# A float32 network on one core: the two token tiles of the stationary pages interleaved word by word

## The chip, the cores and the metric

The kernel runs on one core of one Trainium2 chip. The metric is the device time of one execution in microseconds (us), lower is better. A change of this kernel's time can be told from none from about 2% on.

## The reference, cut to what matters

One sequence of 256 tokens with 1024 channels, all in float32, goes through a state space layer, a causal attention layer, and twice through a mixing layer (latent attention, convolution, retention, gated and merged) and a feed-forward layer. Nearly all the arithmetic is products of the 256 tokens with weight matrices:

```python
h = rms_norm_2(x, ln_mix_pre[l])
proj = h @ w_in[l]                                   # 1024 x 7584
...
merged = gates[:, :, 0] * y_mla + gates[:, :, 1] * y_conv + gates[:, :, 2] * y_ret
x = x + rms_norm_2(merged @ w_out[l], ln_mix_post[l])
h = rms_norm_2(x, ln_ffn_pre[l])
f = (jax.nn.silu(h @ ffn_w_gate[l]) * (h @ ffn_w_up[l])) @ ffn_w_down[l]   # hidden width 2816
x = x + rms_norm_2(f, ln_ffn_post[l])
```

## The kernel before

**Split products.** A float32 operand is split into hi, rounded to the tensor engine's float32r format by ScalarE's copy, and lo, what is left, by a subtraction on VectorE. A product is the sum of three matmuls (`mm3`, lines 163 to 167):

```python
nc.tensor.matmul(out, xh, wh, start=first, stop=False)
nc.tensor.matmul(out, xh, wl, start=False, stop=False)
nc.tensor.matmul(out, xl, wh, start=False, stop=last)
```

The second argument, a block of 128 channels x 128 tokens of the transposed activations, is the stationary operand, which a weight load puts into the array ahead of each matmul. The third, 128 channels x up to 512 columns of a weight matrix, is the moving one, and the result is 128 tokens x 512 columns in PSUM.

**Stationary pages.** `pages` (L214) allots a pair of 4 KB pages (hi, lo) for each four blocks of 128 channels, `[128, 4, 256]`: in each partition 256 tokens follow each other, so a block's 128 tokens of one token tile t are 512 adjacent bytes. The pages are written by `split` (L186 to L194: the hi by ScalarE, L190 or L193, the lo by VectorE, L191 or L194), mostly from `transposed` (L196), which transposes four blocks into PSUM and splits them, with a gain per channel (one split per block, 128 columns wide) or without one (one split for four blocks, 512 wide). `prenorm` (L221) does so with gains at the head of five stages. Names in the trace: xTh/xTl, fh/fl, oTh/oTl, cTh/cTl, mcTh/mcTl, s5mh/s5ml. The state space layer's s5gh/s5gl are pages too, but moving operands (`gemm_t`, L454 to L456); they are written with a step of four words at L844 and L845.

**Weights.** `wtile` (L142) brings 256 x 512 weights by a DMA of 512 KB from SP's queue (raw), splits them (L158 ScalarE, L160 VectorE), and returns a hi and a lo tile. `wbuf` (L135) hands out four buffers of each kind that the whole kernel has, and from the attention stage on two more hi and two more lo that the stage has, by turns.

**Order.** `gemm` (L169) goes through the weight tiles of a product of 512 columns; for each tile it issues 12 matmuls (two token tiles x two k blocks x three), then `pump` runs pieces of side work from queues of closures (attention, convolution taps, retention). `out_rows` (L241) does the same for a product whose 1024 columns are held at once. The unsplit float32 products of the first stage are `gemm_raw` (L428): the trace shows each as two instructions.

Of the kernel before, what the change touches and what calls it, by code (L numbers as in the profile page):

```python
# [23 lines left out]
C = 512  # L24
# [26 lines left out]
class Net:  # L51
# [16 lines left out]
    def stage(self, pages, temps, raws=0, halves=0):  # L68
        """pages and temporaries of a stage; what an earlier stage had is given back."""
# [15 lines left out]
    def page(self, shape, name, dt=F32):  # L85
        """up to 4 KB of each partition"""
        assert int(np.prod(shape[1:])) <= 1024, shape
        return self.bp.tile(shape, dt, tag="q4", name=self.nm(name))
# [46 lines left out]
    def wbuf(self, tag):  # L135
        """buffer of a tile of weights; the stage may have some more of them"""
# [32 lines left out]
    def gemm(self, xs, W, c0, ncols, evac, pts=None):  # L169
        """rows: out[t] = x @ W[:, c0:c0+ncols]; xs: list over k blocks of (hi, lo) aps [128, 256]."""  # L170
        KB = len(xs)
        pts = [self.acc(), self.acc()]
        for k0 in range(0, KB, KT):
            kn = min(KT, KB - k0)
            hi, lo = self.wtile(W[k0 * 128:(k0 + kn) * 128, c0:c0 + ncols], kn, ncols)
            for t in range(2):
                for k in range(kn):
                    xh, xl = xs[k0 + k]
                    s = slice(t * 128, t * 128 + 128)
                    self.mm3(pts[t][:, :ncols], xh[:, s], xl[:, s], hi[:, k, :ncols], lo[:, k, :ncols],  # L180
                             k0 + k == 0, k0 + k == KB - 1)
# [4 lines left out]
    def split(self, dh, dl, src, scale=None):  # L186
        """dh + dl = src * scale, src in PSUM."""
# [8 lines left out]
    def transposed(self, t, row, pages, nb, gains=None, scale=None):  # L196
        """row [128 tok, nb*128] -> split blocks of pages, scaled per channel by gains."""
        nc = self.nc
        for b0 in range(0, nb, 4):
# [4 lines left out]
            s = slice(t * 128, t * 128 + 128)  # L204
            dh, dl = pages[b0 // 4]
            if gains is None:
                self.split(dh[:, :bn, s], dl[:, :bn, s],
                           pt[:, :bn * 128].rearrange("p (b n) -> p b n", b=bn), scale)
            else:
                for b in range(bn):  # L210
                    self.split(dh[:, b, s], dl[:, b, s], pt[:, b * 128:(b + 1) * 128],
                               gains[:, b0 + b:b0 + b + 1])

    def pages(self, nb, name="xT"):  # L214
        return [(self.page([128, min(4, nb - b), 256], name + "h", F32R), self.page([128, min(4, nb - b), 256], name + "l", F32R))
                for b in range(0, nb, 4)]

    def blocks(self, pages):
        return [(h[:, b, :], l[:, b, :]) for h, l in pages for b in range(h.shape[1])]
# [21 lines left out]
    def out_rows(self, xs, W, x, post, out=None):  # L241
        """x + rms(xs @ W) * post, or x + xs @ W when post is None; the first 128 rows are done some tiles ahead."""
# [8 lines left out]
        def product(t, n, k0, kn, hi, lo):  # L251
            s = slice(t * 128, t * 128 + 128)
            for k in range(kn):
                xh, xl = xs[k0 + k]
                self.mm3(pts[t][n], xh[:, s], xl[:, s], hi[:, k, :], lo[:, k, :], k0 + k == 0, k0 + k == KB - 1)
# [36 lines left out]
    def rsqrt1(self, v):  # L292
        """-1024 / 27 / sqrt(v) of a column, by a step of third and one of second order."""
# [16 lines left out]
    # ------------------------------------------------------------------ consts  # L310
# [25 lines left out]
    def sincos(self, out_c, out_s, ang, tag, after=None):  # L336
        """sin and cos of ang (any size that float32 reduces), ang [128, ...]"""
# [18 lines left out]
    def tables2(self):  # L356
# [8 lines left out]
        self.cs = self.sp.tile([128, 2, 2, 80], F32, tag="cs", name="cs", bufs=1)  # (cos/sin, t, mla16|ret64)  # L365
# [5 lines left out]
        # log gammas: min(x, 0) - log1p(exp(-|x|)), log1p by the atanh series  # L371
# [20 lines left out]
        # distances: [m part, mt, n]: relu(n - m), relu(m - n)  # L392
# [9 lines left out]
    # ------------------------------------------------------------------ first block: state space layer  # L402
    def raw_tiles(self, W, c0, ncols, KB):
        """sources of the tiles of gemm_raw, in its order"""
        return [W[k0 * 128:(k0 + KT) * 128, c0 + n0:c0 + n0 + C] for k0 in range(0, KB, KT) for n0 in range(0, ncols, C)]

    def load_raw(self):
        """next tile of self.todo, in any of the buffers of a tile of weights"""
# [6 lines left out]
    def gemm_raw(self, xs, ncols, evac, after=None):  # L415
        """gemm_t on float32 operands that are not split, where the tensor engine has the time: a closure for each tile of self.pre."""
# [22 lines left out]
    def gemm_t(self, xs, W, c0, ncols, evac, order=None):  # L439
        """columns: out^T = W[:, c0:c0+ncols]^T x^T, evac(block, psum [128, 256]); order of the pairs of k blocks."""  # L440
# [20 lines left out]
    def s5_params(self, after):  # L461
# [10 lines left out]
        # powers of ab: [ri, pair, k], k = 0..4  # L472
# [18 lines left out]
        # one chunk further, on (re, -im): [[a, b], [-b, a]] of ab^4  # L491
# [5 lines left out]
        # f = (ab - 1) / (lr + i li)  # L497
# [15 lines left out]
        # sums for products in three multiplications  # L513
# [4 lines left out]
    def s5_bc(self):  # L518
# [4 lines left out]
        # B~ = f B  # L523
# [20 lines left out]
    def s5_pows(self):  # L544
        """powers 1..16 of ab^4: (-im, re, im), pair, power."""
# [19 lines left out]
    def cprod(self, eng, q, l0, Z, Zx):  # L565
        """ab^l z for pairs 8q..8q+7, l = l0..l0+3, as (k1, k2, k3): re = k1 + k3, im = k1 + k2."""
# [14 lines left out]
    def s5_w(self, q, eng):  # L581
        """pairs 8q..8q+7 of ab^k B~, k = 1..4, [(g2, p), qq, (q2, k, c)], pair = 2 qq + q2, re and im."""
# [7 lines left out]
    def s5_wt(self, W, q, w, after=None):  # L590
        """their lhsT [(q2, k, c), qq, (g2, p)]"""
# [8 lines left out]
    def s5_c(self, cab, q, eng):  # L600
        """pairs 8q..8q+7 of [(g2, p), pair, (l, c')] of C ab^l, l = 0..3, re and im."""
# [4 lines left out]
    def s5(self, x_in):  # L606
# [6 lines left out]
        # normalised input; gains go on its channels after the transposes  # L613
# [6 lines left out]
        # gains go on the channels of the input; 1 / rms on what comes out of the first product and on what goes into the second  # L620
# [47 lines left out]
        # block diagonal B~ (re, -im) and the zeros before the kernel taps  # L668
# [55 lines left out]
        # chunk inputs X = W u: [(g2, p), (re, -im), pair, 1 + j], replaced by the states after each chunk  # L724
# [14 lines left out]
        # scan over the 64 chunks: inside 4 groups of 16, across the groups, then what each group takes over  # L739
# [28 lines left out]
        # kernel taps K[l] = Re(C ab^l B~): [(q4, g2, c), pg, (l, c')], channels in order; spread to lower triangles  # L768
# [702 lines left out]
```

## Time and profile before

| what | value |
|---|---|
| runs shown | 1278.69 and 1280.73 us, median 1279.71 |
| span of the profiled execution | 1276.7 us, 3.0 us under the median of the runs |
| TensorE busy (matmuls; weight loads beside them) | 1235.7 us; 1029.5 us |
| VectorE, ScalarE, GpSimd busy | 948.3, 652.9, 51.8 us |
| mean granted TensorE clock | 0.981 |
| HBM read | 205.83 MB, 164 GB/s over the span |

The span goes from the first to the last instruction of the one execution that the profiler recorded. A matmul's recorded duration holds its whole way through the array; the ends are modelled, and matmuls overlap, so their pace is the distance from start to start. PE are the matmuls, PEld the weight loads, DVE is VectorE, ACT ScalarE, POOL GpSimd.

### The profile page before, as it was taken

The numbers are of one execution on the slowest core, as the hardware profiler recorded it, in microseconds if no ns is written. First come the engines' busy times: TensorE is split into PE (matmuls) and PEld (weight loads), VectorE is DVE, ScalarE is ACT, GpSimd is POOL, SyncE is SP. The second block draws the span as 40 slices with busy tenths as digits, with TensorE's granted clock in tenths as the row PEclk, the third lists the DMA queues.
The fourth block names the chain that finished last, engine by engine and source line by source line (L and its number), as shares of the span: only waits on it lengthen the run. The fifth ranks groups of instructions, "written<-read, shape, count | busy, mean of one in ns | idle before, by whom it ended". The sixth has DMA issues, their size and how long they took to land.

```text
span 1276.7 us, 17877 instructions
## 1 busy us (share of the span) xinstructions
PE 1235.7 (97%) x6520; PEld 1029.5 (81%) x6520; DVE 948.3 (74%) x1923; ACT 652.9 (51%) x1073; POOL 51.8 (4%) x42
## 2 busy tenths in 40 slices
PE   7898799999999999999999999999999999999997
PEld 6787777787888888888788887888888887888886
DVE  6999489887889998857755555899998857755544
ACT  3112467675765544544644444666545445644432
POOL 3920000000000000000000000000000000000000
PEclk9779899999999999999999999999999999999999
DMA  9326656644454554555566564544554554665661
GB/s 319 83 43 99 166 174 209 192 136 137 142 164 138 161 161 152 164 201 179 189 180 184 171 235 151 175 134 147 166 159 153 179 184 148 218 190 161 193 211 50
DMA packets 125367, 210.60 MB, mean 165 GB/s; under 512 B 22112, under 2 KB 31328, under 8 KB 125280
## 3 DMA queue, kind: packets, MB, share of 16 engines
q1 hardware_dynamic: 117056, 204.24, 50.9%
q10 hardware_dynamic: 8224, 5.23, 2.1%
q8 instruction: 51, 0.84, 0.3%
q14 instruction: 36, 0.29, 0.1%
HBM read 205.83 MB, written 3.60 MB: 164 GB/s over the span
## 4 chain that ended last, share of the span: by engine, by line
PE 79%; DVE 13%; ACT 3%; DMA 3%; issue 2%; SPq 0%; DVEq 0%; ACTq 0%
PE mm L165 23%; PE mm L167 23%; PE mm L166 22%; DVE lo L160 2%; PE sm L203 2%; ACT hi L158 1%; PE sm L1119 1%; PE sm L1211 1%; DVE cacc L957 1%; PE sm L1094 1%; DVE s5pr L745 1%; PE sm L733 1%; DVE cm L586 1%; DVE s5pr L759 1%; PE mm L455 1%
## 5 line engine op out<-in xcount | busy, mean ns | idle before, releaser
L160 DVE TENSOR_TENSOR lo<-raw,hi 128x1024 fp32r<-128x1024 f32 (+2 forms) x372 | 440.1, 1186 | 235.8 <-ACT hi L158 234.4
L158 ACT ACTIVATE hi<-raw 128x1024 fp32r<-128x1024 f32 (+2 forms) x372 | 382.6, 1032 | 377.8 <-PE mm L167 290.4
L165 PE MATMUL mm<-hi,xTh 128*128 128x512 f32 (+2 forms) x1152 | 451.1, 394 | 1.6 <-ACT xTh L193 1.5
L167 PE MATMUL mm<-hi,xTl 128*128 128x512 f32 (+2 forms) x1152 | 443.7, 386 | 0.3 <-DVE t L297 0.2
L166 PE MATMUL mm<-lo,xTh 128*128 128x512 f32 (+2 forms) x1152 | 443.3, 385 | 0.2 <-DVE lo L160 0.2
L165 PEld LDWEIGHTS mm<-hi,xTh 128*128 128x128 f32 x1152 | 216.4, 188 | 48.9 <-ACT xTh L193 7.3
L167 PEld LDWEIGHTS mm<-hi,xTl 128*128 128x128 f32 x1152 | 216.3, 188 | 46.2 <-DVE t L297 1.5
L166 PEld LDWEIGHTS mm<-lo,xTh 128*128 128x128 f32 x1152 | 216.7, 188 | 41.2 <-DVE lo L160 0.5
L957 DVE SCALAR_TENSOR_TENSOR cacc<-aT,colp,cacc 128x256 f32<-128x256 f32 x240 | 104.2, 476 | 0.0
L165 PE MATMUL mm<-hi,fh 128*128 128x512 f32 x176 | 69.0, 392 | 0.0
L166 PE MATMUL mm<-lo,fh 128*128 128x512 f32 x176 | 68.9, 392 | 0.0
L167 PE MATMUL mm<-hi,fl 128*128 128x512 f32 x176 | 68.8, 391 | 0.0
L167 PEld LDWEIGHTS mm<-hi,fl 128*128 128x128 f32 x176 | 33.0, 187 | 7.4
L165 PEld LDWEIGHTS mm<-hi,fh 128*128 128x128 f32 x176 | 33.0, 188 | 7.3
L166 PEld LDWEIGHTS mm<-lo,fh 128*128 128x128 f32 x176 | 33.0, 188 | 7.2
L277 DVE SCALAR_TENSOR_TENSOR pg<-mm,post 128x512 f32<-128x512 f32 x16 | 11.0, 690 | 21.9 <-ACT pg L275 21.9
L194 DVE SCALAR_TENSOR_TENSOR xTl<-sm,colp,xTh 128x128 fp32r<-128x128 f32 x80 | 24.3, 345 | 3.5 <-ACT xTh L193 3.1
L454 PE MATMUL mm<-s5gh,hi 128*128 128x256 f32 x64 | 19.0, 305 | 7.1 <-ACT s5gh L844 7.1
L193 ACT ACTIVATE xTh<-sm,colp 128x128 fp32r<-128x128 f32 x80 | 24.4, 381 | 1.8 <-DVE xTl L194 1.7
L895 ACT ACTIVATE pg<-mm,t 128x512 f32<-128x512 f32 x24 | 16.5, 690 | 16.9 <-PE mm L167 16.9
L733 PE MATMUL sm<-s5U,s5W 64*64 64x64 f32 x256 | 21.2, 300 | 2.5 <-DMA s5U<-s5ud 2.5
L733 PEld LDWEIGHTS sm<-s5U,s5W 64*64 64x64 f32 x256 | 20.8, 207 | 3.2 <-issue 3.2
(387 smaller groups left out, 1513.2 us busy)
## 6 DMA issues: line engine op xcount, KB each, us to landing
raw<-in_w_in SPq DMA_DIRECT2D x112, 512.0 KB, 3.5
raw<-in_ffn_w_down SPq DMA_DIRECT2D x44, 512.0 KB, 3.8
raw<-in_ffn_w_gate SPq DMA_DIRECT2D x40, 512.0 KB, 3.7
raw<-in_ffn_w_up SPq DMA_DIRECT2D x40, 512.0 KB, 3.6
raw<-in_attn_w_in SPq DMA_DIRECT2D x32, 512.0 KB, 4.3
raw<-in_ret_w_o SPq DMA_DIRECT2D x16, 512.0 KB, 3.2
raw<-in_w_out SPq DMA_DIRECT2D x16, 512.0 KB, 3.2
raw<-in_ssm_w_glu SPq DMA_DIRECT2D x8, 512.0 KB, 4.9
```

Of the source, the lines that this page charges most:

```text
L158: nc.scalar.activation(h, r, AF.Copy)
L160: self.last_lo = nc.vector.tensor_tensor(l, r, h.bitcast(F32), op=ALU.subtract)
L165: nc.tensor.matmul(out, xh, wh, start=first, stop=False)
L166: nc.tensor.matmul(out, xh, wl, start=False, stop=False)
L167: nc.tensor.matmul(out, xl, wh, start=False, stop=last)
L193: a = nc.scalar.activation(dh, src, AF.Copy if isinstance(scale, float) else AF.Identity, scale=scale)
L194: self.last_split = a, nc.vector.scalar_tensor_tensor(dl, src, scale, dh.bitcast(F32), op0=ALU.mult, op1=ALU.subtract)
L203: nc.tensor.transpose(pt[:, b * 128:(b + 1) * 128], row[:, (b0 + b) * 128:(b0 + b + 1) * 128], self.ident)
L454: nc.tensor.matmul(o, wh, xh, start=first and b % 2 == 0, stop=False, skip_group_check=True)
L733: lx[q] = nc.tensor.matmul(pt[g * 64:g * 64 + 64, qq * 64:qq * 64 + 64], Wl[i][h][r, qq, g * 64:g * 64 + 64], U[r, 8 * h + qq, g, :], star ...
L895: nc.scalar.activation(gate[t, n], p, AF.Tanh, scale=hf(t))
L957: nc.vector.scalar_tensor_tensor(cacc[:, b, :], src, sc, cacc[:, b, :], op0=ALU.mult, op1=ALU.add)
```

## The change

A stationary page is now allotted as `[128, nb, 128, 2]` and seen as `[128, nb, 2, 128]`: word 2n of a block is token n of tile 0, word 2n + 1 token n of tile 1. A block of one token tile is 128 words with a step of two words over 1024 bytes, in the weight loads that read it, in ScalarE's and VectorE's writes, and where VectorE reads the hi again. Size and number of the pages are as before. The pages that are moving operands (s5gh, s5gl) keep the old layout by a helper of their own. The rest of the diff removes comments.

```diff
 def gemm(self, xs, W, c0, ncols, evac, pts=None):
...
                 for k in range(kn):
                     xh, xl = xs[k0 + k]
-                    s = slice(t * 128, t * 128 + 128)
-                    self.mm3(pts[t][:, :ncols], xh[:, s], xl[:, s], hi[:, k, :ncols], lo[:, k, :ncols],
+                    self.mm3(pts[t][:, :ncols], xh[:, t], xl[:, t], hi[:, k, :ncols], lo[:, k, :ncols],
                              k0 + k == 0, k0 + k == KB - 1)
...
 def transposed(self, t, row, pages, nb, gains=None, scale=None):
...
-                self.split(dh[:, :bn, s], dl[:, :bn, s],
+                self.split(dh[:, :bn, t], dl[:, :bn, t],
                            pt[:, :bn * 128].rearrange("p (b n) -> p b n", b=bn), scale)
             else:
                 for b in range(bn):
-                    self.split(dh[:, b, s], dl[:, b, s], pt[:, b * 128:(b + 1) * 128],
+                    self.split(dh[:, b, t], dl[:, b, t], pt[:, b * 128:(b + 1) * 128],
                                gains[:, b0 + b:b0 + b + 1])
 
 def pages(self, nb, name="xT"):
-        return [(self.page([128, min(4, nb - b), 256], name + "h", F32R), self.page([128, min(4, nb - b), 256], name + "l", F32R))
-                for b in range(0, nb, 4)]
+        return [(self.stationary(min(4, nb - b), name + "h"), self.stationary(min(4, nb - b), name + "l")) for b in range(0, nb, 4)]
+
+    def stationary(self, nb, name):
+        return self.page([128, nb, 128, 2], name, F32R).rearrange("p b n t -> p b t n")
+
+    def moving(self, nb, name):
+        return [tuple(self.page([128, min(4, nb - b), 256], name + p, F32R) for p in "hl") for b in range(0, nb, 4)]
 
     def blocks(self, pages):
-        return [(h[:, b, :], l[:, b, :]) for h, l in pages for b in range(h.shape[1])]
+        return [(h[:, b], l[:, b]) for h, l in pages for b in range(h.shape[1])]
...
 def out_rows(self, xs, W, x, post, out=None):
...
         def product(t, n, k0, kn, hi, lo):
-            s = slice(t * 128, t * 128 + 128)
             for k in range(kn):
                 xh, xl = xs[k0 + k]
-                self.mm3(pts[t][n], xh[:, s], xl[:, s], hi[:, k, :], lo[:, k, :], k0 + k == 0, k0 + k == KB - 1)
+                self.mm3(pts[t][n], xh[:, t], xl[:, t], hi[:, k, :], lo[:, k, :], k0 + k == 0, k0 + k == KB - 1)
...
 def s5(self, x_in):
...
-        gT = self.pages(8, "s5g")
+        gT = self.moving(8, "s5g")
...
-            mh, ml = (a[:, b % 4, :] for a in mT[b // 4])
-            self.split(mh, ml, m, 0.25)
+            self.split(*(a[:, b % 4] for a in mT[b // 4]), m.rearrange("p (t n) -> p t n", t=2), 0.25)
...
 def conv(self, l, xs, W, hf):
...
-            self.split(cT[0][0][:, 2 * b2:2 * b2 + 2, :], cT[0][1][:, 2 * b2:2 * b2 + 2, :], v)
+            self.split(*(a[:, 2 * b2:2 * b2 + 2] for a in cT[0]), v.rearrange("p b (t n) -> p b t n", t=2))
...
 def mla(self, l, parts):
...
-            self.split(oT[0][0][:, s, :], oT[0][1][:, s, :], pt.rearrange("p (b n) -> p b n", b=2))
+            self.split(oT[0][0][:, s], oT[0][1][:, s], pt.rearrange("p (b t n) -> p b t n", b=2, t=2))
```

## Rows read from the trace of the kernel before

**Rows 1.** The profile page: busy time of each engine (busy us, share of the span, instructions), then the chain that ended last by engine and by line.
```profile
PE 1235.7 (97%) x6520; PEld 1029.5 (81%) x6520; DVE 948.3 (74%) x1923; ACT 652.9 (51%) x1073; POOL 51.8 (4%) x42
...
PE 79%; DVE 13%; ACT 3%; DMA 3%; issue 2%; SPq 0%; DVEq 0%; ACTq 0%
PE mm L165 23%; PE mm L167 23%; PE mm L166 22%; DVE lo L160 2%; PE sm L203 2%; ACT hi L158 1%; PE sm L1119 1%; PE sm L1211 1%; DVE cacc L957 1%; PE sm L1094 1%; DVE s5pr L745 1%; PE sm L733 1%; DVE cm L586 1%; DVE s5pr L759 1%; PE mm L455 1%
```

**Rows 2.** Groups of instructions with shapes kept apart, all of the span: line, engine, operation, out<-in, array tile, out<-in shape, count | busy us, mean ns of one | idle before. L165 alone is shown; L166 and L167 have the same counts.
```profile
L165 PE MATMUL mm<-hi,xTh 128*128 128x512 f32 x1056 | 421.9, 401 | 1.1 <-ACT xTh L193 1.0
...
L165 PE MATMUL mm<-hi,fh 128*128 128x512 f32 x176 | 69.0, 392 | 0.0
...
L165 PE MATMUL mm<-hi,xTh 128*128 128x256 f32 x64 | 18.1, 284 | 0.0
...
L165 PE MATMUL mm<-hi,oTh 128*128 128x512 f32 x32 | 13.1, 410 | 0.0
...
L165 PE MATMUL mm<-hi,s5mh 128*128 128x512 f32 x32 | 12.8, 403 | 0.1
L165 PE MATMUL mm<-hi,cTh 128*128 128x512 f32 x32 | 12.7, 397 | 0.0
...
L165 PE MATMUL mm<-hi,mcTh 128*128 128x512 f32 x16 | 6.3, 391 | 0.0
```

**Rows 3.** Timeline of TensorE from 637 to 654 us, in the first feed-forward stage: start us, us, engine, line, operation, out<-in, array tile, moving shape, count. Of the 70 rows the first, the 46th and the last; the rows between are one matmul each.
```profile
637.49 0.39 PE L165 MATMUL mm<-hi,xTh 128*128 128x512 f32 x1
...
647.69 0.39 PE L165 MATMUL mm<-hi,xTh 128*128 128x512 f32 x1
...
653.29 0.39 PE L165 MATMUL mm<-hi,xTh 128*128 128x512 f32 x1
```

**Rows 4.** The same timeline from 725 to 732 us, where the feed-forward stage's last chunk is 256 columns wide. The first pair of rows is 30 matmuls apart, the second 20.
```profile
725.21 0.28 PE L167 MATMUL mm<-hi,xTl 128*128 128x256 f32 x1
...
728.81 0.28 PE L167 MATMUL mm<-hi,xTl 128*128 128x256 f32 x1
728.92 0.28 PE L165 MATMUL mm<-hi,xTh 128*128 128x256 f32 x1
...
731.19 0.28 PE L167 MATMUL mm<-hi,xTl 128*128 128x256 f32 x1
```

**Rows 5.** Timeline of TensorE from 12 to 17 us, with rows merged: the unsplit float32 products of the first stage (start of the first, us to the end of the last, count). Under it the busy times from 12 to 16 us (start:end, us, busy of PE, PEld, DVE, ACT, POOL with counts, granted clock, DMA share, GB/s).
```profile
12.55 3.62 PE L428 MATMUL mm<-s5x,hi 128*128 128x256 f32 x16
16.00 1.24 PE L428 MATMUL mm<-s5x,lo 128*128 128x256 f32 x5
...
12.00:16.00 4.00, 4.00 (x20) 3.52 (x19) 3.95 (x30) 2.22 (x6) 0.24 (x1) 1.00 1.06 392
```

**Rows 6.** Timeline of all engines near 642 us, the rows of TensorE's matmuls (PE) and weight loads (PEld); under it TensorE alone near 409 us, in the attention of the first mixing stage.
```profile
642.02 0.39 PE L167 MATMUL mm<-hi,xTl 128*128 128x512 f32 x1
642.02 0.19 PEld L165 LDWEIGHTS mm<-hi,xTh 128*128 128x128 f32 x1
642.25 0.39 PE L165 MATMUL mm<-hi,xTh 128*128 128x512 f32 x1
642.25 0.19 PEld L166 LDWEIGHTS mm<-lo,xTh 128*128 128x128 f32 x1
...
408.53 1.00 PE L1119 MATMUL sm<-mv,pg 128*128 128x64 f32 x8
409.37 1.08 PE L1094 MATMUL sm<-mkT,mqT 96*128 96x256 f32 x4
```

**Rows 7.** Busy time of each engine in three stretches (columns as in group 5): all instructions, then those of L165 alone (PE and PEld).
```profile
355.00:500.00 145.00, 144.66 (x725) 120.82 (x724) 136.20 (x277) 82.37 (x136) 0.23 (x2) 1.00 0.49 153
600.00:801.00 201.00, 199.78 (x948) 163.91 (x947) 117.20 (x172) 102.08 (x149) 0.00 (x0) 1.00 0.57 179
801.00:975.00 174.00, 173.85 (x861) 145.51 (x860) 160.55 (x359) 101.94 (x178) 0.00 (x0) 1.00 0.51 159
...
355.00:500.00 145.00, 65.07 (x160) 30.09 (x160) 1.00 0.49 153
...
801.00:975.00 174.00, 80.81 (x201) 37.96 (x202) 1.00 0.51 159
```

**Rows 8.** Timeline of TensorE near 737 us: a group of four transposes between matmuls.
```profile
736.92 0.60 PE L203 MATMUL sm<-first,pg 128*128 128x128 f32 x4
737.27 0.48 PE L165 MATMUL mm<-hi,fh 128*128 128x512 f32 x1
737.59 0.40 PE L166 MATMUL mm<-lo,fh 128*128 128x512 f32 x1
```

**Rows 9.** Groups with shapes kept apart (columns as in group 2): the slowest writes of pages and two usual ones; under them two pieces of the chain in order of time (start us, us, what), from the first attention's prenorm.
```profile
L191 DVE TENSOR_TENSOR xTl<-sm,xTh 128x512 fp32r<-128x512 f32 x12 | 7.8, 684 | 1.3 <-ACT xTh L190 1.2
...
L190 ACT ACTIVATE xTh<-sm 128x512 fp32r<-128x512 f32 x12 | 6.5, 588 | 3.8 <-PE sm L203 3.8
...
L845 DVE TENSOR_TENSOR s5gl<-s5gf,s5gh 128x512 fp32r<-128x512 f32 x4 | 4.5, 1128 | 9.5 <-ACT s5gh L844 9.5
...
L844 ACT ACTIVATE s5gh<-s5gf 128x512 fp32r<-128x512 f32 x4 | 4.5, 1126 | 0.1
...
191.09 1.81 ACT xTh L193 x7
...
193.81 2.16 DVE xTl L194 x8
```

More of the change, by code (lines that the diff above doesn't have):

```diff
@@ L251, in product @@
         def product(t, n, k0, kn, hi, lo):
-            s = slice(t * 128, t * 128 + 128)
             for k in range(kn):
                 xh, xl = xs[k0 + k]
-                self.mm3(pts[t][n], xh[:, s], xl[:, s], hi[:, k, :], lo[:, k, :], k0 + k == 0, k0 + k == KB - 1)
+                self.mm3(pts[t][n], xh[:, t], xl[:, t], hi[:, k, :], lo[:, k, :], k0 + k == 0, k0 + k == KB - 1)
         tiles = [(k0, n) for k0 in range(0, KB, KT) for n in range(2)]
```

## The prediction

> **What bounds the kernel now.** I read the table of busy time and the chain of waits first [rows 1]. TensorE is busy 1235.7 us of the 1276.7, and 79% of the chain that ends last is TensorE, 68% on the three lines of `mm3`. So the end is set by how often one matmul can follow another. The granted clock is 1.00, the 2.4 GHz level, in all stretches used below [rows 5, 7].
>
> The grouped instructions with their shapes give the number of these matmuls [rows 2]: 1056 + 176 + 32 + 32 + 32 + 16 = 1344 on L165 with 512 columns and a stationary page, and the same on L166 and L167: 4032 in all. Their "mean ns" of about 392 is a latency; the pace has to be read from start to start in the timeline. There it has two values that never mix [rows 3]: 45 matmuls from 637.49 to 647.69 us follow each other every 226.7 ns, the next 24 up to 653.29 every 233.3 ns. With a few mixed ones at each change the cycle is 72 long, 48 against 24. A tile of weights serves 12 matmuls and the stage turns six tiles over (four of the whole kernel's, two of its own), so 24 of 72 are the two tiles of the stage's own, hi and lo alike. By the program's allocation these two lie 64 bytes off the 128-byte grid of the other four. The stationary pages meanwhile change (hi or lo, both token tiles, all k) and nothing is seen of it. The mean is (48 x 226.7 + 24 x 233.3) / 72 = 228.9 ns.
>
> What could the pace be? The unsplit float32 products of the first stage show 16 instructions of 256 columns in 3.45 us, 215.6 ns each [rows 5]. So the split matmuls lose 11.1 or 17.7 ns each, 13.3 on the mean, and 4032 x 13.3 = 53.6 us hang on why.
>
> Three readings bear on the why. First, with 256 columns the order of the two kinds turns round [rows 4]: 30 matmuls at 120.0 ns, then 20 at 113.5 on the stage's own tiles. A matmul that only suffered from its own moving address would be longer on the same tiles at either width. A turn-round wants a second stream with a phase of its own, and the only one that runs in step with each matmul is its weight load. Second, the load of the next stationary block starts with the matmul and is over 0.19 us later, before the next start 0.23 us on [rows 6]; its stream proper takes at most 105 ns, since eight loads of 128 columns under matmuls of 64 columns take 0.84 us [rows 6]. So the load hides at 512 columns; it costs only if it disturbs the matmul that it hides under. Third, the bytes: at one column a tick of 2.4 GHz a split matmul sweeps 2048 bytes of each partition in 213.3 ns (9.6 bytes a ns), its load 512 bytes in 105 ns (4.9), so the one overtakes the other. In [rows 5], where nothing is lost, 1024 bytes in 215.6 ns (4.7) run against the same load (4.9): two streams at one speed, which can't run into each other again once apart. But the moving stream there also has half the rate, which excuses it as well.
>
> **The change, part by part.**
>
> *Weight loads* (4032 at 512 columns). The two token tiles lie word by word in turn, so a block's 128 words span 1024 bytes. If the load keeps its pace, it sweeps 9.7 bytes a ns, the speed of the moving stream above it. Bounds for the pace of a pair: 215.6 ns, nothing left of the loss [rows 5], and as much again as now, 228.9 + 13.3 = 242.2 ns, if each load disturbs in proportion to the bytes that it spans. No row has a load with a step of two words. I take the side of [rows 5], the only pairs at equal speed: gain up to 53.6 us.
> What of it reaches the end? In 355 to 500 and 801 to 975 us VectorE is busy 136.2 of 145 and 160.6 of 174 us [rows 7], by the taps and softmaxes queued there; 3 x (160 + 201) = 1083 matmuls run there, 14.4 us of the gain, and I give half to VectorE's being late next. The rest is 2949 x 13.3 = 39.2 us; VectorE and ScalarE have 40% idle in such a stretch (117.2 and 102.1 of 201) and the weights' DMA share is 0.57, so they can follow. 39.2 + 7.2 = 46.4. A load may still run into the matmul once at its start, whose phase nobody chose: I take off a fifth, 37.
>
> *Loads where they don't hide.* At 256 columns (64 on each line, 192, [rows 2]) the pace is 113 to 120 ns against a load of 105, and after a group of transposes the first load comes close behind them: from 736.92 to 737.59 us four transposes and one matmul take 670 ns, so some 443 are the group's [rows 8]. If the load keeps its speed, nothing changes. If a step of two words halved it, to 210 ns: 192 x 95 = 18.2 us, and up to 105 ns a group; L203's 2% of the chain [rows 1] are 25.5 us or 58 groups, 6.1 us, and the other lines that transpose may double that to 12.2. I take nothing; 30 us stay as a bound.
>
> *Writes of the pages.* ScalarE's hi and VectorE's lo now write, and VectorE reads, every second word. The nearest rows are L844 and L845, whose pages are written with a step of four words: 1126 ns against 588 for L190, 1128 against 684 for L191 [rows 9], about 1 ns a column. The full price on 52 splits of 512 columns and 92 of 128 would be some 40 us on each engine, but nearly all of it under matmuls. On the path are the splits of a prenorm, eight of each engine in the first [rows 9], 1.81 and 2.16 us, that is 16 x 0.12 = 2 us more in each of five, 10 in all; the floor is 0. Two words of step are nearer to one than to four in what they skip: I take 2 us.
> The Trainium skill says of this (SBUF — State Buffer, Specifications) that SBUF has 16-byte lines and that two hits in a line suffice for full speed. Four words of step are one float32 hit in a line and two words are two, so by it the writes would cost 0 instead of 2 us. The slow L844 agrees; no run here shows the step of two.
>
> *Nothing else moves*: the same tiles, buffers, queues and waits; `gT`, a moving operand, keeps its layout (`moving`).
>
> Sum for the profiled execution: 1276.7 - 37 + 2 = 1241.7 us; the shown runs' median lies 3.0 us above this span, so 1244.7, say **1245**. Its own range is 1226 (all 53.6) to 1262.
>
> **Rivals.**
>
> *No change* (1280; 1276 to 1290). The loss is the moving stream's own, as a plain cost of streaming at 9.6 bytes a ns, and the load's layout doesn't enter. For it: all stationary addresses give one pace. Against it: [rows 4] turn the order round. The time is 1279.7 plus 0 to 10 us of writes.
> The Trainium skill has this rival as a rule (TensorE: Matmul & The Clock Gate, Part 2): weights load through a read port of their own and take no bandwidth from the running matmul. Rows 3 and 4 speak against it, since the pace hangs on a pair of addresses.
>
> *The clash doubles* (slower, 1306 to 1333). The loads' toll is per piece of memory touched: a block touches twice the pieces and each costs the running matmul the same. For it: the loss doesn't grow with the columns, at one column a tick 256 columns take 106.7 ns and 512 take 213.3, which leaves 13.3 of the 120.0 and 13.4 of the 226.7, so it comes by the load. Against it: [rows 5] with the same loads lose nothing. Price: 13.3 ns more x 4032 = 53.6 us, half of it 26.8: 1333 or 1306. It decides from 6.3 ns a matmul, a mean pace of 235 ns, where 25.6 us are reached.
>
> *The load halves* (slower, 1310). The bound above, 30 us, with the pace at 512 columns as it is, since 210 ns still fit under 226.7. For it: L844 shows that a step can cost a factor of two. Against it: that step is twice as long.
>
> **How the numbers follow.** The streams at one speed: 0.47. No change: 0.31. The clash doubles: 0.13. The load halves: 0.09. A measurement here tells about 2%, 25.6 us, so faster means under 1254, slower over 1305. The forecast is over the bound in all but some 0.03 of its 0.47; of the slower ones, all but 0.01 are. Faster 0.44, same 0.35, slower 0.21. Range 1226 to 1312: below it some 0.05, above it some 0.13.
>
> **What would show it.** Right: paces of 215 to 220 ns in the long runs, the difference between the tiles gone or shrunk; the load's 188 ns unchanged; matmuls' share of the chain lower, VectorE's higher between 355 and 500 us; L193 and L194 within 20 ns of before. Wrong: 226.7 and 233.3 again (no change); 235 or more (clash); 200 ns and more at 256 columns (halved load); L190 near 1 us (writes).

## The result, and the profile after

The changed kernel takes 1289.4 us against 1279.7: 1.0076 of the time before, with a 95% interval of 1.0047 to 1.0106. I had forecast 1245, 35 us less; it became some 10 us slower. The interval lies above 1, but 0.8% is under the 2% from which a change is told from none here. The profiled span is 1287.4 us, 10.7 more than before. In the profile page (busy time, then the chain by engine and by line) TensorE is 10.2 us busier than in [rows 1] and its share of the chain has gone up by one point.

```profile
PE 1245.9 (97%) x6520; PEld 1054.6 (82%) x6520; DVE 946.1 (73%) x1923; ACT 655.0 (51%) x1073; POOL 41.5 (3%) x42
...
PE 80%; DVE 13%; ACT 3%; DMA 2%; issue 2%; SPq 0%; ACTq 0%; DVEq 0%
PE mm L165 23%; PE mm L166 23%; PE mm L167 23%; PE sm L202 2%; DVE lo L160 2%; DVE s5pr L750 1%; PE sm L1123 1%; PE sm L1215 1%; ACT hi L158 1%; DVE cacc L961 1%; PE sm L1098 1%; DVE s5X L755 1%; DVE cm L591 1%; DVE s5pr L764 1%; PE mm L460
```

The paces have moved, the wrong way. In the timeline of TensorE, where [rows 3] had 226.7 and 233.3 ns by turns, the two rows below are 66 matmuls apart: 15.39 us, 233.2 ns each, over all six tiles of weights. At 256 columns, where [rows 4] had 120.0 and 113.5, 59 matmuls lie between the two rows, 120.0 ns each. So the difference between the tiles has gone, as forecast, but both kinds now stand at the slower of the two old levels.

```profile
639.43 0.39 PE L165 MATMUL mm<-hi,xTh 128*128 128x512 f32 x1
...
654.82 0.40 PE L165 MATMUL mm<-hi,xTh 128*128 128x512 f32 x1
```

```profile
729.83 0.28 PE L166 MATMUL mm<-lo,xTh 128*128 128x256 f32 x1
...
736.91 0.28 PE L165 MATMUL mm<-hi,xTh 128*128 128x256 f32 x1
```

The groups with shapes kept apart show the writes and the load: VectorE's write of a page takes 686 ns (684 in [rows 9]), ScalarE's 622 (588), and the weight load 194 ns (188 before).

```profile
L190 DVE TENSOR_TENSOR xTl<-sm,xTh 128x512 fp32r<-128x512 f32 x12 | 7.8, 686 | 1.4 <-ACT xTh L189 1.3
...
L189 ACT ACTIVATE xTh<-sm 128x512 fp32r<-128x512 f32 x12 | 6.9, 622 | 3.8 <-PE sm L202 3.8
...
L165 PEld LDWEIGHTS mm<-hi,xTh 128*128 128x128 f32 x1152 | 224.0, 194 | 45.1 <-ACT xTh L192 7.1 <-ACT xTh L189 0.5
```

Where do the 10.7 us arise? The first product on split operands starts at 139.23 us before and at 138.15 after (first row of the timeline of each that has it: start, duration, count, idle time ahead):

```profile
139.23 1.01 PE L454 MATMUL mm<-s5gh,hi 128*128 128x256 f32 x3 [7.08 <-ACT s5gh L844]
```

```profile
138.15 1.01 PE L459 MATMUL mm<-s5gh,hi 128*128 128x256 f32 x3 [7.21 <-ACT s5gh L849]
```

So the change is 1.1 us ahead there, which is within the scatter (138.15 to 141.80 in the eight traces of the network alone). Behind it the kernel takes 1149.3 us against 1137.5, 11.8 more. For the mean pace, here and in the table further down, I took the mean of all distances from start to start between 512-column matmuls of `mm3` that follow each other within 260 ns (some 3770 of them in each trace): 229.75 ns before, 232.87 after. By kind of tile (as the stage's own count those that the first experiment's padding speeds up), the whole kernel's four went from 228.2 to 233.1 and the stage's own two from 232.7 to 232.4. The 4032 matmuls times 3.12 ns are 12.6 us. Nothing else is needed to explain the result, and nearly all of the pace reached the end.

### The profile page after: what moved, and what is told of

Its sections match the earlier page's. It is cut to its first block, busy times and chain, and to the rows that moved or that the text cites. A ratio compares the mean times of both kernels' runs of the same rounds, so it can differ in the third digit from the quotient of the medians.

```text
span 1287.4 us, 17877 instructions
## 1 busy us (share of the span) xinstructions
PE 1245.9 (97%) x6520; PEld 1054.6 (82%) x6520; DVE 946.1 (73%) x1923; ACT 655.0 (51%) x1073; POOL 41.5 (3%) x42
## 4 chain that ended last, share of the span: by engine, by line
PE 80%; DVE 13%; ACT 3%; DMA 2%; issue 2%; SPq 0%; ACTq 0%; DVEq 0%
PE mm L165 23%; PE mm L166 23%; PE mm L167 23%; PE sm L202 2%; DVE lo L160 2%; DVE s5pr L750 1%; PE sm L1123 1%; PE sm L1215 1%; ACT hi L158 1%; DVE cacc L961 1%; PE sm L1098 1%; DVE s5X L755 1%; DVE cm L591 1%; DVE s5pr L764 1%; PE mm L460 1%
## 5 line engine op out<-in xcount | busy, mean ns | idle before, releaser
L165 PE MATMUL mm<-hi,xTh 128*128 128x512 f32 (+2 forms) x1152 | 454.0, 396 | 1.6 <-ACT xTh L192 1.4
L167 PE MATMUL mm<-hi,xTl 128*128 128x512 f32 (+2 forms) x1152 | 446.5, 388 | 0.2
L166 PE MATMUL mm<-lo,xTh 128*128 128x512 f32 (+2 forms) x1152 | 446.5, 388 | 0.2 <-DVE lo L160 0.2
L165 PEld LDWEIGHTS mm<-hi,xTh 128*128 128x128 f32 x1152 | 224.0, 194 | 45.1 <-ACT xTh L192 7.1
L167 PEld LDWEIGHTS mm<-hi,xTl 128*128 128x128 f32 x1152 | 223.9, 194 | 42.0 <-DVE t L302 1.4
L166 PEld LDWEIGHTS mm<-lo,xTh 128*128 128x128 f32 x1152 | 224.0, 194 | 37.6 <-DVE lo L160 0.5
L165 PE MATMUL mm<-hi,fh 128*128 128x512 f32 x176 | 69.5, 395 | 0.0
L167 PE MATMUL mm<-hi,fl 128*128 128x512 f32 x176 | 69.4, 394 | 0.0
L166 PE MATMUL mm<-lo,fh 128*128 128x512 f32 x176 | 69.4, 394 | 0.0
L167 PEld LDWEIGHTS mm<-hi,fl 128*128 128x128 f32 x176 | 34.2, 194 | 6.8
L165 PEld LDWEIGHTS mm<-hi,fh 128*128 128x128 f32 x176 | 34.2, 194 | 6.7
L166 PEld LDWEIGHTS mm<-lo,fh 128*128 128x128 f32 x176 | 34.2, 194 | 6.7
L433 PE MATMUL mm<-s5x,lo 128*128 128x256 f32 x80 | 23.8, 455 | 0.0
L1393 ACT ACTIVATE pg<-mm,t 128x512 f32<-128x512 f32 (+1 forms) x24 | 15.6, 651 | 14.9 <-PE mm L167 14.9
```

The source lines that it names most:

```text
L433: self.last_raw = nc.tensor.matmul(o, raw[:, k, b * 128:b * 128 + 128], xs[k0 + k], start=k0 + k == 0 and b % 2 == 0, stop=k0 + k == len(x ...
```

## The experiments

Three kernels have a section behind the network that runs 48 matmuls from each line and nothing beside them; a pace there is the distance of two lines' starts, divided by 48 (96 for float32, which takes two records a matmul). The same runs as a program of their own gave no result. `S(b, k)` is a stationary operand that begins at byte b and takes every k-th word, `M(b, n)` a moving one of n columns from byte b; both tiles begin on the same place of the 256-byte grid. The place of an operand is its address modulo 256 bytes.

**Do the two paces come from the 64 bytes?**

```diff
+ self.ctx0.enter_context(self.tc.tile_pool(name=self.nm("pd"), bufs=1)).tile([128, 16], F32, name=self.nm("pd"))
  self.sp = self.ctx0.enter_context(self.tc.tile_pool(name=self.nm("sp"), bufs=2))
```

> The kernel before, with 64 bytes of padding ahead of the stage's second pool, so that its own two tiles of weights lie on the 128-byte grid like the other four. Nothing else is changed. If the moving address sets which of the two paces holds: all runs at 226.7 ns, 1332 matmuls of 512 columns 6.7 ns shorter, 8.9 us less, 1271. If the two paces come from the tiles' being the stage's own (their place far up in the memory, their writers) and not from the 64 bytes: 1280 and 233.3 as before on those tiles.

Measured: 1272.5 us, 0.9946 of before (0.9933 to 0.9960). In the first feed-forward stage the timeline has no slow stretch left; 27 matmuls lie between these rows, 226.7 ns each.

```profile
645.30 0.39 PE L168 MATMUL mm<-hi,xTl 128*128 128x512 f32 x1
...
651.42 0.39 PE L168 MATMUL mm<-hi,xTl 128*128 128x512 f32 x1
```

The moving operand's address sets the pace. This kernel is also faster than both, by less than the 2%.

**Step, address and place, one at a time.**

```diff
+ for p, s, v, a, z in seg(9, [S(0), S(512)], [M(128), M(2176)]): nc.tensor.matmul(p, s, v, start=a, stop=z)
...
+ for p, s, v, a, z in seg(20, [S(64), S(576)], [M(64), M(2112)]): nc.tensor.matmul(p, s, v, start=a, stop=z)
```

> The kernel before with a section behind it that only runs matmuls on split-type (float32r) operands, 48 from each line, with one thing changed at a time, to be read as paces from start to start; the time of the whole has some 650 us more and is not looked at. The first lines repeat the kernel before (stationary step of one word, 512 columns): 226.7 ns at a moving address on the 128-byte grid and 233.3 at 64 bytes off it, as in the network. Theory A (a toll for each piece of memory that the load touches): the pace grows with the step, 233 at two words, about 247 at four, 273 at eight; 64 columns of the stationary at two words cost what 128 at one word cost. Theory B (the place of the load against the moving stream decides, the step only takes the place away): 233 at every step from two words on; stationary and moving both 64 bytes off give 226.7 again, the stationary alone off gives 233. Theory C (the load itself becomes slower): at 64 and 128 columns of moving data, where the load doesn't hide, the pace is some 6 ns longer at two words, and about double at four. At 256 columns A and B expect 120 on the grid and 113 off it at a step of one, and 120 at two, as the network showed.

The timeline, one row for each line (start, from the first start to the last end, count). L1489 has the stationary at 0 and the moving tile at 64 bytes: (1343.39 - 1332.39) / 48 = 229.2 ns. L1493 to L1495 have the stationary at 0 and the moving tile at 128, 192 and 256 bytes: (1387.93 - 1376.78) / 48 = 232.3, then 233.3 and 227.1 ns. L1504 and L1505 have the moving tile at 64 and the stationary at 64 and 96: 227.5, 233.1 ns.

```profile
1332.39 11.16 PE L1489 MATMUL mm<-mv,st 128*128 128x512 f32 x48
1343.39 11.25 PE L1490 MATMUL mm<-mv,st 128*128 128x512 f32 x48
...
1376.78 11.32 PE L1493 MATMUL mm<-mv,st 128*128 128x512 f32 x48
1387.93 11.36 PE L1494 MATMUL mm<-mv,st 128*128 128x512 f32 x48
1399.13 11.06 PE L1495 MATMUL mm<-mv,st 128*128 128x512 f32 x48
1410.03 11.05 PE L1496 MATMUL mm<-mv,st 128*128 128x512 f32 x48
...
1498.82 11.08 PE L1504 MATMUL mm<-mv,st 128*128 128x512 f32 x48
1509.74 11.35 PE L1505 MATMUL mm<-mv,st 128*128 128x512 f32 x48
1520.93 11.37 PE L1506 MATMUL mm<-mv,st 128*128 128x512 f32 x48
```

So the difference of the two addresses decides, with a period of 256 bytes: 226.7 ns in steady run at equal places, 228.8 to 234.4 at all others but one of those tried in steps of 16 bytes or more (the stationary 16 bytes off: 226.7). That is theory B at a step of one. Theory A fell: four words of step took 235.0 and 239.3 ns where it wanted 247, eight took 244.3 and 245.4 where it wanted 273; both are over B's 233 too. Theory C's runs stood mostly at a granted clock of 0.50; those of the second of the three kernels, further down, decide on it.

Two forecasts from the network missed. The moving tile at 64 bytes takes 229.2 ns, not 233.3; at 192 bytes, which is also 64 off the 128-byte grid, it takes 233.3. So the grid is one of 256 bytes, not of 128 as I had it, and the stage's own tiles run at the pace of the second of these places; at which they stood is not on record. At 256 columns the two addresses gave 120.0 and 117.8, not 113.5: the turn-round of [rows 4] is there, but its size isn't reproduced.

**All weights off the place, no stride.**

```diff
+ pool("pa", 1).tile([128, 16], F32, name="pa")
  self.wp = pool("wp", 4)
+ pool("pb", 1).tile([128, 16], F32, name="pb")
```

> The kernel before, with two paddings of 64 bytes that move all six tiles of weights 64 bytes off the 128-byte grid and leave the stationary pages on it. The pages are as before, not by turns. If the whole loss of the change is the pace's other level: 2700 matmuls of 512 columns go from 226.7 to 233.3 ns, up to 18 us more, less what hides, so about what the change gives, 1289 to 1298, with no strided load or write. If the strided loads or writes cost more than the level: this kernel stays clearly below the changed one's 1289.4.

Measured: 1290.6 us, 1.0094 (1.0077 to 1.0111), mean pace 233.3 ns. Two paddings of 64 bytes, with nothing strided, cost as much as the change, as far as the runs tell (the intervals overlap).

**A good place with two words, and the load's part.**

```diff
+ for p, s, v, a, z in seg(2, [S(0,2), S(4,2)], [M(0), M(2048)]): nc.tensor.matmul(p, s, v, start=a, stop=z)
...
+ for p, s, v, a, z in seg(36, [S(0,1,32), S(512,1,32)], [M(0), M(2048)]): nc.tensor.matmul(p, s, v, start=a, stop=z)
```

> Again the kernel before with a section behind it that only runs matmuls, 48 from each line, to be read as paces; the time of the whole is not looked at. What is known by now: at a step of one word the pace of 512 columns hangs on the difference of the two operands' addresses, with 226.7 ns at a multiple of 256 bytes and up to 233 at others. Theory B (a step of two words takes the good place away): 233 at all 16 differences of 16 bytes that are tried with two words. Rival B2 (with two words there is a good place too, at another difference): at least one of the 16 gives 226.7, and the change could be had without its loss by a shift. Theory D (what is left over 213.3 ns at the best place, 13.4 ns, is the weight load's toll): with 32 columns of the stationary it falls to some 217. Rival E (it belongs to the split type's stream, whatever the load does): 226.7 to 233 with 32 columns too; the unsplit float32 with 256 columns, two passes, takes 215.6 as in the first stage, at any difference and with two words alike. Where the load doesn't hide, 64 columns of moving data: 112 ns with one word, 118 with two, 233 with four.

The same timeline. L1490 (one word, equal places) is the control: 226.7 ns. L1491, the same moving tile under a stationary with two words: 233.3. L1500 is the best of the 16 differences with two words: (1411.74 - 1400.65) / 48 = 231.0. L1507 is one word again: 227.9 with its first mixed ones. L1522, four words: 239.4. L1525, 32 columns of the stationary at equal places: 231.3. L1527, every other load with two words, all at place 0: 230.2. L1564, float32 with two words of step and 256 columns: 20.72 us / 96 = 215.8.

```profile
1289.18 11.04 PE L1490 MATMUL mm<-mv,st 128*128 128x512 f32 x48
1300.06 11.36 PE L1491 MATMUL mm<-mv,st 128*128 128x512 f32 x48
1311.26 11.36 PE L1492 MATMUL mm<-mv,st 128*128 128x512 f32 x48
...
1400.65 11.25 PE L1500 MATMUL mm<-mv,st 128*128 128x512 f32 x48
1411.74 11.35 PE L1501 MATMUL mm<-mv,st 128*128 128x512 f32 x48
...
1478.82 11.10 PE L1507 MATMUL mm<-mv,st 128*128 128x512 f32 x48
1489.76 11.37 PE L1508 MATMUL mm<-mv,st 128*128 128x512 f32 x48
...
1646.58 11.66 PE L1522 MATMUL mm<-mv,st 128*128 128x512 f32 x48
1658.07 11.65 PE L1523 MATMUL mm<-mv,st 128*128 128x512 f32 x48
...
1680.99 11.27 PE L1525 MATMUL mm<-mv,st 128*32 128x512 f32 x48
1692.09 11.29 PE L1526 MATMUL mm<-mv,st 128*32 128x512 f32 x48
1703.22 11.21 PE L1527 MATMUL mm<-mv,st 128*128 128x512 f32 x48
1714.27 11.36 PE L1528 MATMUL mm<-mv,st 128*128 128x512 f32 x48
...
2066.07 20.88 PE L1564 MATMUL mm<-mv,st 128*128 128x256 f32 x96
2086.79 10.52 PE L1565 MATMUL mm<-mb,sb 128*128 128x512 bf16 x47
```

The same loads by themselves (groups, mean ns of one): 312 ns with four words, 193 with two, 188 with one, 109 for 32 columns.

```profile
L1522 PEld LDWEIGHTS mm<-mv,st 128*128 128x128 f32 x48 | 11.6, 312 | 0.0
...
L1491 PEld LDWEIGHTS mm<-mv,st 128*128 128x128 f32 x48 | 9.3, 193 | 1.9
...
L1490 PEld LDWEIGHTS mm<-mv,st 128*128 128x128 f32 x48 | 9.0, 188 | 1.9
...
L1525 PEld LDWEIGHTS mm<-mv,st 128*32 128x32 f32 x48 | 5.2, 109 | 5.8
```

Where the load doesn't hide, under 64 columns of moving data (one, two and four words of step; granted clock 1.00 in all three stretches; a last matmul's own 0.28 us, 0.40 in the third, is taken off): 3.24 us / 29 = 111.7 ns, 2.71 / 23 = 117.8, 2.56 / 11 = 232.7.

```profile
1942.75 3.52 PE L1554 MATMUL mm<-mv,st 128*128 128x64 f32 x30
...
1970.73 2.99 PE L1557 MATMUL mm<-mv,st 128*128 128x64 f32 x24
...
2001.30 2.96 PE L1560 MATMUL mm<-mv,st 128*128 128x64 f32 x12
```

B stands and B2 fell: with two words none of 16 places gives 226.7, they take 231.0 to 233.4. One rival to the step itself is the place of the second token tile, whose blocks begin 4 bytes further, and with one word a shift of 4 bytes loses the good place as well (L1515, 236.6). L1527 speaks against it: its blocks with two words begin at place 0, every other one is plain, and the pace lies halfway between 226.7 and 233.3. So the step alone is enough to take the good place away. D fell: a load of a quarter of the columns doesn't make the pair faster, it even loses the good place. E is right on 32 columns and on float32. Theory C is right as well, in a small size: a load with two words takes 6 ns more, one with four takes twice.

**Does the good place still matter in the changed kernel?**

The edit is that of the first experiment, in the changed kernel.

```diff
+ self.ctx0.enter_context(self.tc.tile_pool(name=self.nm("pd"), bufs=1)).tile([128, 16], F32, name=self.nm("pd"))
```

> The changed kernel with the 64 bytes of padding that brought all six tiles to the best place in the kernel before (1272.5 there). If a step of two words takes the good place away: nothing happens, 1289.4 within 2 us, all six tiles at 233.3 ns. If the difference of the addresses still decided: the stage's own two tiles, a third of the matmuls, would change their pace, by up to 9 us.

Measured: 1292.7 us, 1.0107 of before (1.0090 to 1.0124), a mean of 233.4 ns on both kinds of tile. Nothing is won, as the first reading has it. The 3.3 us over 1289.4 are more than the 2 I allowed. The pace explains a part: in the changed kernel the stage's own tiles stood at 232.4 ns. But in the profiled execution the first split product starts at 141.80 us, 3.7 later than in the changed kernel, and behind it this kernel takes 1150.0 us against 1149.3. So in that execution most of the difference lies ahead of the matmuls that the padding bears on.

**What of the moving stream is slow?**

```diff
+ for p, s, v, a, z in seg(2, [S(0), S(512)], [M(0,1).to_broadcast([128, 512]), M(2048,1).to_broadcast([128, 512])]): nc.tensor.matmul(p, s, v, start=a, stop=z)
...
+ for p, s, v, a, z in seg(20, [S(0,t=sb16), S(512,t=sb16)], [M(0,512,2,t=mb16), M(4,512,2,t=mb16)]): nc.tensor.matmul(p, s, v, start=a, stop=z)
```

> Again the kernel before with runs of 48 matmuls behind it, to be read as paces; the time of the whole is not looked at. What is known by now: bfloat16 with 512 columns and passes of float32 with 256 columns take 215.8 ns; split-type pairs 226.7 ns at the best place and 231 to 233 at nearly all others, also with 32 columns of the stationary. What is asked is what of the moving stream makes the split type 11 to 18 ns slower. Theory F (the memory that it sweeps, 4 bytes a column at one column a tick): a split-type moving tile that is one word repeated 512 times sweeps none and takes 215.8 to 218 at any place and any step of the stationary; bfloat16 with a step of two elements sweeps as much as the split type and takes 226 to 233; a split-type moving tile with a step of two words sweeps twice and takes 240 or more. Theory G (the type itself, whatever it sweeps): 226.7 to 233 with the repeated word too, and 215.8 for bfloat16 with a step of two.

The timeline: L1492, the split type with one word repeated, 215.8 ns; L1493, the same 192 bytes off, L1497 with two words of stationary step: 215.8 too. L1494, a moving step of two words: (1342.42 - 1320.68) / 48 = 452.9. L1509, bfloat16: 216.0; L1510, bfloat16 with every second element: 226.0.

```profile
1299.96 10.52 PE L1492 MATMUL mm<-mv,st 128*128 128x512 f32 x48
1310.32 10.52 PE L1493 MATMUL mm<-mv,st 128*128 128x512 f32 x48
1320.68 21.93 PE L1494 MATMUL mm<-mv,st 128*128 128x512 f32 x48
1342.42 21.94 PE L1495 MATMUL mm<-mv,st 128*128 128x512 f32 x48
...
1375.10 10.52 PE L1497 MATMUL mm<-mv,st 128*128 128x512 f32 x48
1385.46 10.52 PE L1498 MATMUL mm<-mv,st 128*128 128x512 f32 x48
...
1558.35 10.53 PE L1509 MATMUL mm<-mb,sb 128*128 128x512 bf16 x48
1568.72 11.00 PE L1510 MATMUL mm<-mb,sb 128*128 128x512 bf16 x48
1579.57 11.04 PE L1511 MATMUL mm<-mb,sb 128*128 128x512 bf16 x48
```

All forecasts of theory F came true, and G fell. A moving operand that repeats one word loses nothing, at either place and over loads of one word, of two words and of 32 columns (L1502, 215.8). bfloat16 that is made to advance 4 bytes a column takes 226.0, the split type's best pace, though its loads are half as long in the record (96 ns). So 10.9 ns (226.7 - 215.8) come only with a moving operand that advances at least 4 bytes a column, and no load tried takes them away.

But F's picture of a price on each byte swept isn't borne out. Four words of step (L1507, 459.8 ns) take hardly more than two. And at 4 bytes a column the loss doesn't grow with the columns. With the operands at equal places, 256 columns take 120.0 ns, 384 take 173.3 (L1525 of the first of the three kernels), 512 take 226.7.

```profile
1698.88 8.49 PE L1525 MATMUL mm<-mv,st 128*128 128x384 f32 x48
1707.20 8.48 PE L1526 MATMUL mm<-mv,st 128*128 128x384 f32 x48
```

That is 0.417 ns a column, one tick of the 2.4 GHz level (granted clock 1.00 in all three), and the rest is the same for each matmul. (448 columns took 202.6 and 206.4 and 480 took 216.7, 3 to 6 ns above this line, so the good place hangs on the width too.) A loss that comes once a matmul may still have to do with the load, of which each matmul here has one beside it. Whether the 10.9 ns would stay without a load is not shown.

**Writes alone, loads alone, and their control.** A page's stretch is now written by both token tiles in all three, so the kernels share one order of instructions and one set of waits.

The edits are in `pages`, `blocks` and `transposed` of the changed kernel: a page `a` stays [128, nb, 256], and what `split` writes and what the matmuls read are two views of it.

```diff
+ ps.append(tuple(a.rearrange("p b (n t) -> p b t n", t=2) for a in pair))
+ ps.read.append(tuple(a.rearrange("p b (t n) -> p b t n", t=2) for a in pair))
```

> The changed kernel with its pages still written by turns, as in the change, but read by the matmuls in plain blocks, as before; so the products get permuted numbers. It prices the strided writes by themselves, and the waits that a page's now shared stretch may bring. If writes with a step of two words cost nothing: 1279 within 3 us, paces 226.7 and 233.3 as before. By my prediction's term: 2 us more, 10 at most.

```diff
+ ps.append(tuple(a.rearrange("p b (t n) -> p b t n", t=2) for a in pair))
+ ps.read.append(tuple(a.rearrange("p b (n t) -> p b t n", t=2) for a in pair))
```

> The other half: pages written in plain blocks as before, but read by the matmuls by turns, so again on permuted numbers. If the loads alone make the difference: 1289 to 1291, the time of the changed kernel, with 233.3 ns on all six tiles. If a part of the change's loss comes with the writes: 1280 to 1287.

```diff
+ ps.append(tuple(a.rearrange("p b (t n) -> p b t n", t=2) for a in pair))
+ ps.runs.append(tuple(a.rearrange("p b (h t n) -> p b t h n", h=2, t=2) for a in pair))
+ ps.read.append(tuple(a.rearrange("p b (t n) -> p b t n", t=2) for a in pair))
...
+ dh, dl = pages.runs[b0 // 4]
```

> The control for the two halves, on permuted numbers like them: pages read in plain blocks, and written in two runs of 64 neighbouring words for each token tile and block, so that nothing is strided, but each block that a matmul reads was written in part by both token tiles, as in the two halves; the instructions stand in the order of the halves. What the two halves lose together by this waiting for the other token tile is then seen alone. If strided writes cost nothing: 1291.5 within 2 us, the time of the half with the strided writes. If strided writes cost my prediction's term: 1289.5; its upper bound: 1281.5. The half with the strided loads (1304.2) then lies 12.7 us above, which is the price of the loads.

Measured against before: writes alone 1.0100 (1.0086 to 1.0115), 1291.5 us; loads alone 1.0202 (1.0186 to 1.0217), 1304.2; control 1.0095 (1.0078 to 1.0112), 1292.0. Writes alone and loads alone both missed their forecasts, by some 13 us: it looked like a cost of the writes, which no duration supports. TensorE's waits tell what it is. At the start of a stage it transposes the second token tile after a gap of up to 3.8 us, three times and 11.3 us in all (us in total, times, longest; writes alone, then control; loads alone has 11.2),

```profile
PE sm L208 <- DVE x L303: 11.3, 3, 3.8
```

```profile
PE sm L217 <- DVE x L313: 11.3, 3, 3.8
```

while the changed kernel has the first tile's matmuls in that place and no gap ahead of its transposes at 612.03:

```profile
608.49 0.51 PE L165 MATMUL mm<-hi,xTh 128*128 128x512 f32 x1 [0.29 <-ACT xTh L192]
...
612.03 0.60 PE L202 MATMUL sm<-first,x 128*128 128x128 f32 x4
```

A block that both tiles write in part can't be read before both are there. The change doesn't have this, since every second word belongs to one tile alone. The control takes it out. Against the runs of the kernel before that were taken beside each, writes alone is 13.1 us slower, loads alone 25.8 and the control 12.8. So strided writes cost 0.3 us, which can't be told from nothing or from 2, and strided loads 13.0. ScalarE's write is longer by 35 ns with the stride (622 against 587), with no effect on the time that these runs could show.

The pace prices all of these kernels to within 3 us (mean of each trace as above):

| kernel | mean pace, ns | 4032 x difference, us | measured, us |
|---|---|---|---|
| all six tiles at the good place | 227.62 | -8.6 | -6.6 |
| before | 229.75 | 0 | 0 |
| the change | 232.87 | +12.6 | +9.7 |
| no stride, all six off the place | 233.32 | +14.4 | +11.8 |
| the change, with the padding | 233.36 | +14.6 | +14.2 |
| loads alone, against the control (229.73) | 232.91 | +12.8 | +13.0 |

## Why the prediction was wrong

*The bound* was right: the end hangs on the distance between matmuls, and 3.12 ns on each of 4032 came out at the end. My discount for stretches where VectorE is nearly full is not tested by a loss, since nobody has to keep up with a slower TensorE. The one gain measured, with the 64 bytes of padding, brought 6.6 of 8.6 us, 0.77, where I allowed 0.87 (46.4 of 53.6).

*The step that failed* is the one from "a second stream takes part" to "two streams at one speed can't clash", the term of -37 us. It holds two errors. First the size of what could be won: I put all 13.3 ns down to the load, since the unsplit pairs lose nothing over the same loads. I wrote beside it that their moving stream has half the rate, "which excuses it as well", and didn't price that excuse. It is the larger part: 10.9 ns come with a moving operand of 4 bytes a column, and no layout of the stationary that was tried goes below 226.7. What address and load could still give was 229.75 - 226.7, some 3 ns or 12 us, and the 64 bytes of padding took 6.6 of it. (The prediction's 228.9 is the mean of one steady stretch; over the whole trace it is 229.75.) Second the sign: the load does take part, but by its place against the moving tile. With a step of one word equal places are good, and four of six tiles happened to have them; with a step of two no place tried is. The change took the good place from two thirds of the matmuls: 226.7 to 233.3 in a steady stretch, 228.2 to 233.1 over the whole trace, which is the mean's 3.1.

*The turn-round at 256 columns* [rows 4] was rightly read as a sign of the second stream, and wrongly as a sign that all of the loss came with it. A row that shows that two things interact doesn't show that nothing remains without the interaction.

*Loads that don't hide* at nothing, *writes* at 2 us: right to within their bounds. A load with two words takes 6 ns more, not 95, and the writes cost 0.3 us, within the noise; the 10 us of their bound are out. The Trainium skill's rule (SBUF — State Buffer, Specifications) that two hits in a 16-byte line suffice agrees for the load, with 118 ns for two words and 233 for four against 112 for one, and for the writes, with 622 and 686 ns for two words against 588 and 684 for one and 1126 and 1128 for four. For the moving stream the measurement differs: two words of step are two hits too, and it takes 453 ns for 227.

*The rivals.* "No change" put the loss on the moving stream, which is right of the larger part in so far as it needs 4 bytes a column; a plain cost of streaming would grow with the columns, and it doesn't. Its 1276 to 1290 holds 1289.4 by luck: the layout does enter, and costs the 10 us that it had for the writes. "The clash doubles" had the sign, and was right that the loss doesn't grow with the columns. It asked for 6.3 ns a matmul; it was 6.7 in steady stretches on the tiles that had the good place, 3.1 on the mean. A toll for each piece of memory touched fell with theory A. "The load halves" needs four words.
The Trainium skill's rule that loads take no bandwidth from the running matmul (TensorE: Matmul & The Clock Gate, Part 2) doesn't carry over to the pace: L1490 and L1491 differ in the load's step alone, 226.7 and 233.3 ns. Its 215.7 ns for 512 columns back to back (the section "Wait — 56ns, not 53.3ns?") agrees with bfloat16 here (216.0) and not with the split type (226.7 at best).

*What stays open*: why equal places are good, and of the others tried with one word only the stationary 16 bytes further; why 32 columns of the stationary lose them; what the 10.9 ns once a matmul consist of; and why the stage's own tiles took 113.5 ns at 256 columns [rows 4]. The runs show on what they hang, not the circuit.

## What to carry to other kernels

When a pace is over its floor, ask of each stream by itself whether it explains the gap, and price the excuse you are about to set aside: one run in which the moving operand repeats a word would have shown that 10.9 of 13.3 ns hang on the moving operand. Where float32r matmuls of 512 columns bound the kernel, put both operands on the same place of the 256-byte grid: 64 bytes of padding gave 0.5% here. And a kernel that splits a change in halves can bring a wait of its own: give it a control with the same waits.

## What was not expected of the hardware

- A split-type moving operand with a step of two words takes 452.9 ns for 512 columns, twice its plain pace, and one with four words 459.8; a stationary one with two words takes 118 for 112, and doubles only at four.
- A load with four words takes 309 to 312 ns in the record instead of 188 and still hides nearly whole under 512 columns: 235 to 240 ns.
- A shift of 4 bytes between moving and stationary operand is enough to lose the good place: 236.6 ns, the slowest pace of any offset tried with one word.
